# A hybrid decoder layer: another form for VectorE's two-tile operations, other durations for the planner's clocks

## The chip, the cores and the metric

The kernel runs on one core of a Trainium2 chip. A core has five engines that run side by side, each through its own queue in order: TensorE (PE, with its weight loads PEld), VectorE (DVE), ScalarE (ACT), GpSimd (POOL) and SyncE (SP, which here only issues transfers). They wait for each other through semaphores. The metric is the time of one execution on the device in microseconds (us), lower is better.

## The reference, cut to what matters

One layer for 256 tokens of width 2048, in float32. `rms_norm(x)` goes through one wide projection, whose columns feed two mixers; their outputs are merged by sigmoid gates, projected, and followed by a dense FFN of width 5632.

```
xn = rms_norm(h, ln_mix);  proj = xn @ w_in
q, k, v, z, b, a, sc_b, sc_c, sc_h, gate_a, gate_b = split(proj)
o_a = rms_norm(gated_delta(l2(silu(conv4(q,k))), silu(conv4(v)), decay(a), sigmoid(b))) * silu(z)
o_b = sc_b * conv3(sc_c * sc_h)
h = h + (sigmoid(gate_a) * (o_a @ w_proj_a) + sigmoid(gate_b) * (o_b @ w_proj_b)) @ w_out
h = h + (silu(rms_norm(h) @ w_gate) * (rms_norm(h) @ w_up)) @ w_down
return rms_norm(h, ln_final)
```

The gated delta rule (16 heads of 128) needs, in each head, the inverse of a unit-triangular matrix over the tokens.

## The kernel before, in words

**Products.** Every weight matrix is read once, in groups of 128 x 1024 numbers (two k-tiles of 512 columns). A group `raw` is loaded by SyncE; ScalarE makes its high part `wh` (a cast to float32r), VectorE the low part `wl = raw - wh`; a product is then three matmuls (hi x wh, lo x wh, hi x wl) for each k-tile and each of two token halves. So a group of weights feeds 12 matmuls of 512 columns, here called products; `wh63` is group 63 and feeds products 756 to 767, counted from the start. A projection of 512 columns is 96 products (`mm_k`, `mm_q`, ...), a result in two banks of PSUM. `ensure` makes the groups three ahead of their use.

**Order.** TensorE first makes k, q, v for head group 0, then for each further group k, the z of the group before, q, v; then the short convolution's scc, sch, scb (with z3 behind scc0), the gates and projections, out, and the FFN. What has to happen to a result (`post_qk`, `post_v`, `core`, ...) is written as generators that stop at every dependent step. `step` (line 329), called twice in each group of weights, runs those steps whose due time has come by the planner's own clocks. These are in `Pace` (line 52): one clock for each engine, advanced by an assumed duration for each instruction recorded through `Lane` (line 141) and by what its operands wait for. So the assumed durations decide behind how many products a step stands in each queue. They decide nothing on the chip: there an instruction waits in its queue until its semaphores allow it. When two results are still pending at the start of a product, `product` (line 372) forces steps ahead of their due time, whatever the clocks say, until one is evacuated.

**The DeltaNet steps of a head group** (four heads; the names carry the group's number). k and q are evacuated as rows, flipped to channels by 16 transposes on VectorE (fc), convolved (cv, 12 operations of VectorE), split into kh and kl, squared and split again (scv by ScalarE, sfc by VectorE), and summed by eight matmuls (ssb). Then, in `core` (line 809): the gram matmuls `gr0`, `gr1`, masked by VectorE into `ua`; the blocks of the diagonal are copied by ScalarE (c32), written to DRAM and read back in another layout by GpSimd's transfers (d0, ub); GpSimd inverts 32 x 32 blocks by forward substitution in 62 small operations (tb, rb); the result goes out and back (d1, rc); ScalarE copies rc into R, VectorE transposes parts of it (mt), and two levels of matmuls z and y complete the inverse. Then come u, uc, o, and oc, whose output `oa` is one mixer's result. Line 538, `hop`, issues the transfers, on GpSimd's queue.

**The end of the stage.** The evacuation of scb1 (`post_b`, line 1079) waits for the last oc, since its tiles take over memory of the DeltaNet stage.

Of the kernel before, what the change touches and what calls it, by code (L numbers as in the profile page):

```python
# [13 lines left out]
ALU = mybir.AluOpType  # L14
# [3 lines left out]
D = 2048  # L18
# [19 lines left out]
HOPE = 1  # L38
HOP = 2500.0
NOW = -2  # L40
# [11 lines left out]
class Pace:  # L52
    """Estimated engine clocks (ns), from each instruction's cost and the data it waits for."""

    RATE = {"act": (95.0, 0.84), "dve": (62.0, 1.045), "pool": (100.0, 2.25)}
    TABLE = {AF.Exp: 1, AF.Ln: 2, AF.Sigmoid: 3, AF.Silu: 4}
# [71 lines left out]
class Slots:  # L128
    """A tile pool that tells the clocks which tile takes over which slot."""

# [10 lines left out]
class Lane:  # L141
# [3 lines left out]
    def __getattr__(self, name):  # L145
        f = getattr(self.eng, name)
        pace, key = self.pace, self.key

        def call(*a, **k):
            aps = [v for v in (*a, *k.values()) if hasattr(v, "tensor")]  # L150
            out = k["out"] if "out" in k else a[0]
            outs = [out] + ([k["accum_out"]] if "accum_out" in k else [])
            ins = [v for v in aps if not any(v is o for o in outs)]
            n = math.prod(out.shape[1:])
            if name == "dma_start":
                pace.issue(key, 60.0, outs[:1], aps[1:], lag=HOP)
                return f(*a, **k)
            if key == "pe":
                rows = ins[0].shape[-1]
                if name == "transpose":  # L160
                    cyc = 2 * n
                elif ins[0].dtype == F32R:
                    cyc = max(n, 2 * rows)
                else:
                    cyc = 4 * max(n, rows, 32)
                pace.issue(key, cyc / 2.4 + 3.0, outs, ins)
                return f(*a, **k)  # L167
            if name == "tensor_reduce":
                n = math.prod(ins[0].shape[1:])
            cost, rate = Pace.RATE[key]  # L170
            if key == "pool" and name == "scalar_tensor_tensor":
                rate = 1.4
            cost += rate * n
            if key == "dve" and any(v.space == bass.MemoryType.PSUM for v in aps):
                cost += Pace.PSUM_COST
            if any(hasattr(k.get(nm), "tensor") for nm in ("scale", "scalar", "scalar1")):
                cost += Pace.SCALAR_COST
            func = a[2] if name == "activation" and len(a) > 2 else None
            table = Pace.TABLE.get(func, pace.table)
            if table != pace.table:  # L180
                pace.table = table
                cost += 1300.0
            pace.issue(key, cost, outs, ins)
            return f(*a, **k)  # L184

        return call
# [3 lines left out]
def tile_gdn_shortconv_layer(  # L190
# [23 lines left out]
    pace = Pace()  # L214
# [32 lines left out]
    def fetch(dst, src, free=0.0):  # L247
        """Load on the weights' queue."""
        nc.sync.dma_start(dst, src)
        start = max(pace.t["dma"], free)  # L250
        pace.t["dma"] = start + 4.0 * math.prod(dst.shape) / 360.0
        pace.note(dst, "dma", True, pace.t["dma"] + Pace.DMA_LAG)

    def pair(pool, tag, nm):
        t = pool.tile([P, 2, HG, T], F32R, tag=tag, name=nm)
        return t[:, 0], t[:, 1]

# [1 line left out]
    order = []  # L259
# [22 lines left out]
    def ensure(i, part=KGRP):  # L282
        while nxt[0] <= min(i, len(groups) - 1):
            n = nxt[0]
# [8 lines left out]
            for js in cuts:  # L293
                act.copy(wh[:, js, :], raw[:, js, :])
                if n < EARLY:
                    dve.tensor_tensor(wl[:, js, :], raw[:, js, :], wh[:, js, :], op=ALU.subtract)
                    continue
                lows.append((wl, raw, wh))
                if len(lows) > LOWLAG:
                    wl_, raw_, wh_ = lows.pop(0)  # L300
                    dve.tensor_tensor(wl_, raw_, wh_, op=ALU.subtract)
            ready[n] = (wh, wl)
            nxt[0] += 1
            if nxt[0] == len(groups):
                for wl_, raw_, wh_ in lows:
                    dve.tensor_tensor(wl_, raw_, wh_, op=ALU.subtract)

# [103 lines left out]

# [1 line left out]
    g_mix = const.tile([P, KD], F32, name="g_mix")  # L413
# [36 lines left out]
    def split(hi, lo, src, scale=None):  # L450
        if scale is None:
            act.copy(hi, src)
            dve.tensor_tensor(lo, src, hi, op=ALU.subtract)
        else:
            act.activation(hi, src, AF.Copy, scale=scale)
            dve.scalar_tensor_tensor(
                out=lo, in0=src, scalar=scale, in1=hi, op0=ALU.mult, op1=ALU.subtract
            )
# [65 lines left out]

# [1 line left out]

# [122 lines left out]
    def post_qk(g, qk, pt, me):  # L649
# [27 lines left out]
        yield  # L677
        dve.tensor_tensor(kq[1][:, :, qk, :], y, kq[0][:, :, qk, :], op=ALU.subtract)
        yield
# [6 lines left out]
        yield  # L686
        dve.tensor_tensor(sq[1], y, sq[0], op=ALU.subtract)
        yield 1
# [81 lines left out]
    def decay(g):  # L770
# [3 lines left out]

        # decay between token pairs, keys on partitions
        up_b = upper.unsqueeze(1).broadcast_to([P, HG, P])
# [32 lines left out]
    def core(g):  # L809
# [7 lines left out]

        # [keys, head, (kk, qk), block, queries]
        ua = gp.tile([P, HG, 2, 3, P], F32, tag="ua", name=f"ua_{g}")
# [33 lines left out]
        mark(("gram", g))  # L853
        # inverses of the unit-triangular 32-blocks: one block's every fourth row to a partition
        NM = 2 * HG
# [195 lines left out]

# [1 line left out]
    ob = [None] * NS  # L1053
# [25 lines left out]
    def post_b(n, pt, me):  # L1079
# [12 lines left out]
        yield from flip(rows, ch)  # L1092
        dve.tensor_tensor(y, y, ch, op=ALU.mult)
        yield SOON
# [23 lines left out]

# [1 line left out]
    while not late:  # L1120
# [8 lines left out]
    def post_m(n, br, pt, sg):  # L1129
        for m in range(2):  # L1130
            if br == 0:
                dve.tensor_tensor(mg[n][:, m, :], pt[m], sg[:, m, :], op=ALU.mult)
            else:
                dve.tensor_tensor(sg[:, m, :], pt[m], sg[:, m, :], op=ALU.mult)
                dve.tensor_tensor(mg[n][:, m, :], mg[n][:, m, :], sg[:, m, :], op=ALU.add)
        close(pt)
# [21 lines left out]

# [1 line left out]
    hg = [pair(apool, f"a{n}", f"hg{n}") for n in range(NS)]  # L1160
# [30 lines left out]

# [1 line left out]
    ff = []  # L1193
# [37 lines left out]
    def rsqrt_last(s0, s1, part, m):  # L1231
        """1 / sqrt(part + (s0 + s1) / D), one number to a partition."""
        t, h, y, u = (small.tile([P, 1], F32, tag=f"ry{i}", name=f"ry{i}{m}") for i in range(4))
# [17 lines left out]
    def post_y(n, m, pt):  # L1251
# [11 lines left out]
        if n < NS - 1:  # L1263
            dve.tensor_tensor(xh[:, m, cs], xh[:, m, cs], fin, op=ALU.mult)
            if n == NS - 2:
# [96 lines left out]
```

## Time and profile before

| | us |
|---|---|
| three runs | 1926.2, 1926.51, 1927.36 (median 1926.51) |
| span of the profiled execution | 1926.3 |
| TensorE busy | 1875.3 (97%) |
| VectorE busy | 1322.0 (69%) |
| ScalarE busy | 951.6 (49%) |
| GpSimd busy | 197.3 (10%) |

The profile tells of the profiled execution no time but its span, 0.2 us below the median of the runs. Busy TensorE is counted by the union of its matmuls, which overlap: one product is shown as 0.39 us long, while the next starts 0.23 us later. Idle time in front of an instruction is shown in brackets behind a row of a timeline, with what ended it; "L184" is the line of the helper that records every operation, so rows are told apart by their tiles, `out<-in`. In a timeline, neighbouring instructions of one kind are merged into one row (x2, x16).

### The profile page before, as it was taken

Reading aid. Unit: us, or ns where it says so; the run is one execution under the profiler, and the core shown is the slowest. Engines: PE = TensorE matmul, PEld = TensorE weight load, DVE = VectorE, ACT = ScalarE, POOL = GpSimd, SP = SyncE. Lnnn points to the kernel's source line nnn. Section 1 sums busy time; section 2 is a strip of 40 time slices with the busy share of each in tenths; the row PEclk is TensorE's granted clock in tenths of the full one; section 3 lists DMA queues with packets and bytes.
Section 4 is the critical chain, followed back from the end, with each engine's and each line's share of the span. In section 5 each row is a group of like instructions: output and inputs, shape, how many; then the busy total and the mean of one; then the engine's idle time right before and its main releaser. Section 6 shows DMA issues by size and latency. Waiting matters only on the chain.

```text
span 1926.3 us, 23591 instructions
## 1 busy us (share of the span) xinstructions
PE 1875.3 (97%) x8590; PEld 1543.4 (80%) x8590; DVE 1322.0 (69%) x1923; ACT 951.6 (49%) x1264; POOL 197.3 (10%) x352
## 2 busy tenths in 40 slices
PE   9999899997979999999999999999999999999998
PEld 7887687886867888888888888888888888888886
DVE  6899687896856778544466688766666666644454
ACT  6756766766544444444444444544444444444433
POOL 0007145172450000000000000000000000000000
PEclk9999999998989999999999999999999999999999
DMA  8556354363444655666655555566655555565553
GB/s 305 175 164 192 134 161 154 121 199 107 153 159 131 205 192 188 221 200 205 189 196 194 191 193 179 184 199 205 195 191 194 195 195 189 186 223 192 192 190 132
DMA packets 100357, 354.87 MB, mean 184 GB/s; under 512 B 12177, under 2 KB 12433, under 8 KB 99985
## 3 DMA queue, kind: packets, MB, share of 16 engines
q1 hardware_dynamic: 98432, 349.69, 55.1%
q0 software_dynamic: 1664, 3.67, 0.7%
q8 instruction: 67, 1.10, 0.2%
q14 instruction: 50, 0.40, 0.1%
q10 hardware_dynamic: 144, 0.01, 0.0%
HBM read 350.18 MB, written 3.15 MB: 183 GB/s over the span
## 4 chain that ended last, share of the span: by engine, by line
PE 80%; POOL 6%; issue 4%; DVE 4%; DMA 3%; ACT 2%; SPq 0%; POOLq 0%; DVEq 0%; ACTq 0%
PE mm_dn L167 13%; PE mm_fg L167 12%; PE mm_fu L167 12%; PE mm_proj L167 9%; PE mm_gate L167 9%; PE mm_out L167 5%; PE mm_scb L167 3%; PE mm_sch L167 3%; POOL tb L184 3%; PE mm_z L167 3%; POOL rb L184 2%; PE mm_q L167 2%; PE mm_scc L167 2%; PE mm_k L167 2%; PE mm_v L167 2%
## 5 line engine op out<-in xcount | busy, mean ns | idle before, releaser
L184 DVE TENSOR_TENSOR wl<-raw,wh 128x1024 fp32r<-128x1024 f32 (+1 forms) x652 | 793.1, 1229 | 503.7 <-ACT wh L184 498.8
L184 ACT CAST wh<-raw 128x1024 fp32r<-128x1024 f32 (+1 forms) x652 | 680.7, 1047 | 806.4 <-PE mm_fu L167 132.3
L167 PE MATMUL mm_dn<-wh,ff 128*128 128x512 f32 x704 | 219.0, 392 | 0.0
L167 PE MATMUL mm_fg<-wh,hg 128*128 128x512 f32 x704 | 216.7, 389 | 0.0
L167 PE MATMUL mm_fu<-wh,hg 128*128 128x512 f32 x704 | 216.7, 389 | 0.0
L167 PE MATMUL mm_gate<-wh,xg 128*128 128x512 f32 x512 | 157.6, 389 | 0.0
L167 PEld LDWEIGHTS mm_dn<-wh,ff 128*128 128x128 f32 x704 | 132.4, 188 | 29.5
L167 PEld LDWEIGHTS mm_fg<-wh,hg 128*128 128x128 f32 x704 | 132.2, 188 | 27.4
L167 PEld LDWEIGHTS mm_fu<-wh,hg 128*128 128x128 f32 x704 | 132.2, 188 | 27.3
L167 PE MATMUL mm_dn<-wl,ff 128*128 128x512 f32 x352 | 138.0, 392 | 0.0
L167 PE MATMUL mm_fg<-wl,hg 128*128 128x512 f32 x352 | 136.9, 389 | 0.0
L167 PE MATMUL mm_fu<-wl,hg 128*128 128x512 f32 x352 | 136.9, 389 | 0.0
L167 PEld LDWEIGHTS mm_gate<-wh,xg 128*128 128x128 f32 x512 | 96.1, 188 | 20.1
L167 PE MATMUL mm_gate<-wl,xg 128*128 128x512 f32 x256 | 99.7, 389 | 0.0
L167 PE MATMUL mm_z<-wh,xg 128*128 128x512 f32 x256 | 83.8, 409 | 0.0
L167 PE MATMUL mm_sch<-wh,xg 128*128 128x512 f32 x256 | 81.4, 399 | 0.0
L167 PE MATMUL mm_k<-wh,xg 128*128 128x512 f32 x256 | 79.4, 391 | 0.9 <-ACT wh L184 0.8
L167 PE MATMUL mm_out<-wh,m 128*128 128x512 f32 x256 | 80.1, 394 | 0.0
L167 PE MATMUL mm_proj<-wh,ob 128*128 128x512 f32 x256 | 79.9, 393 | 0.0
L167 PE MATMUL mm_q<-wh,xg 128*128 128x512 f32 x256 | 79.9, 393 | 0.0
L167 PE MATMUL mm_scc<-wh,xg 128*128 128x512 f32 x256 | 79.8, 393 | 0.0
L167 PE MATMUL mm_v<-wh,xg 128*128 128x512 f32 x256 | 79.2, 390 | 0.0
(247 smaller groups left out, 2879.6 us busy)
## 6 DMA issues: line engine op xcount, KB each, us to landing
raw<-in_w_in_dram SPq DMA_DIRECT2D x284, 512.0 KB, 4.2
raw<-in_w_gate_dram SPq DMA_DIRECT2D x88, 512.0 KB, 4.2
raw<-in_w_up_dram SPq DMA_DIRECT2D x88, 512.0 KB, 4.1
raw<-in_w_down_dram SPq DMA_DIRECT2D x88, 512.0 KB, 4.3
raw<-in_w_pb_dram SPq DMA_DIRECT2D x32, 512.0 KB, 4.3
raw<-in_w_pa_dram SPq DMA_DIRECT2D x32, 512.0 KB, 4.2
raw<-in_w_out_dram SPq DMA_DIRECT2D x32, 512.0 KB, 3.6
raw<-in_w_in_dram SPq DMA_DIRECT2D x8, 256.0 KB, 6.4
```

The source lines that it names most:

```text
L167: return f(*a, **k)
L184: return f(*a, **k)
```

## The change

There are two parts. First, where VectorE combined two tiles by a TENSOR_TENSOR operation in SBUF at the named places (wl above all, kl, sfc, the low parts of `split`, and three others), it now gets SCALAR_TENSOR_TENSOR with the constant 1.0 as its scalar: out = (a * 1.0) op b. Second, the planner's clocks get other durations: a transfer issued on GpSimd's queue occupies it for 650 ns instead of 60 and takes 3200 instead of 2500 ns more to land; GpSimd's operations 268 + 2.6 n ns instead of 100 + 2.25 n; VectorE's transposes 187 + 1.02 n instead of 62 + 1.045 n; memsets a rate of their own; a product 226.5 instead of 216.3 ns. What is computed stays the same.

```diff
-HOP = 2500.0
+HOP = 3200.0
+HOP_ISSUE = 650.0
-    RATE = {"act": (95.0, 0.84), "dve": (62.0, 1.045), "pool": (100.0, 2.25)}
+    RATE = {"act": (95.0, 0.84), "dve": (62.0, 1.045), "pool": (268.0, 2.6)}
+    TRANSPOSE = (187.0, 1.02)
+    MEMSET = (100.0, 0.86)
...
-                pace.issue(key, 60.0, outs[:1], aps[1:], lag=HOP)
+                pace.issue(key, HOP_ISSUE, outs[:1], aps[1:], lag=HOP)
...
-                pace.issue(key, cyc / 2.4 + 3.0, outs, ins)
+                pace.issue(key, cyc / 2.26, outs, ins)
...
-            if key == "pool" and name == "scalar_tensor_tensor":
-                rate = 1.4
+            if key == "dve" and name == "transpose":
+                cost, rate = Pace.TRANSPOSE
+            if name == "memset":
+                cost, rate = Pace.MEMSET
...
+    def both(out, a, b, op):
+        dve.scalar_tensor_tensor(out=out, in0=a, scalar=1.0, in1=b, op0=ALU.mult, op1=op)
+    def rest(lo, src, hi):
+        both(lo, src, hi, ALU.subtract)
...
-                    dve.tensor_tensor(wl_, raw_, wh_, op=ALU.subtract)
+                    rest(wl_, raw_, wh_)
...
-        dve.tensor_tensor(kq[1][:, :, qk, :], y, kq[0][:, :, qk, :], op=ALU.subtract)
+        rest(kq[1][:, :, qk, :], y, kq[0][:, :, qk, :])
...
-        dve.tensor_tensor(sq[1], y, sq[0], op=ALU.subtract)
+        rest(sq[1], y, sq[0])
...
-        dve.tensor_tensor(y, y, ch, op=ALU.mult)
+        both(y, y, ch, ALU.mult)
```

The second part moves instructions. The first z of head group 0 on TensorE stood before between weight groups 63 and 64; the last gr of that group stands in front of product 528 (group 44).

```order
L167 MATMUL mm0_k2_1766<-wl63_1871,xg3_135 128x512
L167 MATMUL mm1_k2_1767<-wh63_1870,xg3_135 128x512 x2
L167 MATMUL mm1_k2_1767<-wl63_1871,xg3_135 128x512
L167 MATMUL z_0_0_1995<-mt_141,ua_0_1279 32x32 x8
L167 MATMUL z_0_1_2006<-mt_141,ua_0_1279 32x32 x8
L167 MATMUL mm0_z1_2017<-wh64_1893,xg0_132 128x512 x2
L167 MATMUL mm0_z1_2017<-wl64_1894,xg0_132 128x512
```

The same place on TensorE in the changed program, where the last gr of the group stands in front of product 540 (group 45):

```order
L170 MATMUL mm0_q2_2204<-wl73_2083,xg0_132 128x512
L170 MATMUL mm1_q2_2205<-wh73_2082,xg0_132 128x512 x2
L170 MATMUL mm1_q2_2205<-wl73_2083,xg0_132 128x512
L170 MATMUL z_0_0_2230<-mt_141,ua_0_1297 32x32 x8
L170 MATMUL z_0_1_2241<-mt_141,ua_0_1297 32x32 x8
L170 MATMUL mm0_q2_2204<-wh73_2082,xg0_132 128x512 x2
L170 MATMUL mm0_q2_2204<-wl73_2083,xg0_132 128x512
```

So z moved from product 768 to product 882, the middle of group 73. Counted in the same way, the products between the last gr of a head group and its first z go from 240, 240, 246 and 234 to 342, 324, 294 and 312.

The sums of k3's squares, ssb_k3, on TensorE: before they stood inside scc0, in front of product 1452, with gr of head group 2 ending in front of product 1314.

```order
L167 MATMUL mm1_scc0_4009<-wl120_3943,xg0_132 128x512
L167 MATMUL ssb_k3_4029<-scv_k3_3987,sel_121 32x256 x4
L167 MATMUL ssb_k3_4029<-sfc_k3_3988,sel_121 32x256 x4
L167 MATMUL mm0_scc0_4008<-wh121_3962,xg0_132 128x512 x2
L167 MATMUL mm0_scc0_4008<-wl121_3963,xg0_132 128x512
```

In the changed program they stand between two results, with gr of head group 2 ending in front of product 1434:

```order
L170 MATMUL mm1_scc0_3893<-wl127_3989,xg3_135 128x512
L170 MATMUL ssb_k3_4155<-scv_k3_4151,sel_121 32x256 x4
L170 MATMUL ssb_k3_4155<-sfc_k3_4152,sel_121 32x256 x4
L170 MATMUL mm0_z3_4176<-wh128_4075,xg0_132 128x512 x2
L170 MATMUL mm0_z3_4176<-wl128_4076,xg0_132 128x512
```

They are now at product 1536, the last product of scc0 ahead of them and the first of z3 behind.

What feeds ssb_k3, on VectorE before, from the end of k3's convolution:

```order
L184 SCALAR_TENSOR_TENSOR cv_k3_3881<-fc_k3_3701,wc_123,cv_k3_3881 128x253 x2
L184 TENSOR_TENSOR wl119_3918<-raw119_3916,wh119_3917 128x1024
L184 TENSOR_TENSOR wl120_3943<-raw120_3941,wh120_3942 128x1024
L184 TENSOR_TENSOR kl_3_3699<-cv_k3_3881,kh_3_3698 128x4x256
L184 TENSOR_TENSOR wl121_3963<-raw121_3961,wh121_3962 128x1024
L184 TENSOR_TENSOR wl122_3982<-raw122_3980,wh122_3981 128x1024
L184 TENSOR_TENSOR sfc_k3_3988<-cv_k3_3881,scv_k3_3987 128x1024
```

And the same steps on VectorE in the changed program:

```order
L189 SCALAR_TENSOR_TENSOR cv_k3_3993<-fc_k3_3887,wc_123,cv_k3_3993 128x253 x2
L189 SCALAR_TENSOR_TENSOR wl129_4100<-raw129_4098,wh129_4099 128x1024
L189 SCALAR_TENSOR_TENSOR wl130_4125<-raw130_4123,wh130_4124 128x1024
L189 SCALAR_TENSOR_TENSOR kl_3_3885<-cv_k3_3993,kh_3_3884 128x4x256
L189 SCALAR_TENSOR_TENSOR sfc_k3_4152<-cv_k3_3993,scv_k3_4151 128x1024
```

The two wl between kl and sfc are gone from there. ScalarE's square of cv_k3 and its copy scv_k3 lie between kl and sfc in both programs.

Three other places: in GpSimd's queue the two multiplications of zs_2 now stand between the transfers d1_1 and rc_1 (before behind rc_1), and those of zs_3 between d1_2 and rc_2; the start of sch2 follows o1_3 on TensorE directly, with the evacuation of scc2 behind ScalarE's squares of o1_3; and the last oc, oc_3_1, moves from product 2010 to product 2250. Behind that TensorE's order is as before.

## Rows read from the trace of the kernel before

**Rows 1.** The page's first line.
```profile
span 1926.3 us, 23591 instructions
```
**Rows 2.** Busy time by stretch: stretch, length, engines' busy us, TensorE's clock, DMA.
```profile
0.00:604.40 604.40, 562.51 (x2831) 461.59 (x2832) 473.29 (x862) 379.14 (x654) 197.34 (x352) 0.97 0.50 166
604.40:1917.00 1312.60, 1312.60 (x5760) 1081.85 (x5759) 844.60 (x1046) 570.88 (x606) 0.00 (x0) 1.00 0.59 193
...
150.00:200.00 50.00, 46.43 (x209) 37.17 (x207) 47.96 (x79) 28.00 (x42) 36.52 (x75) 1.00 0.61 194
```
**Rows 3.** Chain that ended last: start us, us, what.
```profile
604.37 21.76 PE mm_scb L167 x96
```
**Rows 4.** Timeline of TensorE: start us, us, what [idle before, what ended it].
```profile
139.00 0.28 PE L167 MATMUL gr<-kl,kh 128*128 128x256 f32 x1
...
203.33 0.32 PE L167 MATMUL z<-mt,ua 128*32 128x32 f32 x2 [5.48 <-DVE mt L184]
...
206.15 1.22 PE L167 MATMUL mm_z<-wh,xg 128*128 128x512 f32 x2
...
208.88 0.76 PE L167 MATMUL dec<-gd,lower_r 128*128 128x512 f32 x2
...
261.49 0.28 PE L167 MATMUL gr<-kl,kh 128*128 128x256 f32 x1
...
322.29 0.28 PE L167 MATMUL z<-mt,ua 128*32 128x32 f32 x2 [2.95 <-DVE mt L184]
...
379.86 0.28 PE L167 MATMUL gr<-kl,kh 128*128 128x256 f32 x1
...
447.66 0.28 PE L167 MATMUL z<-mt,ua 128*32 128x32 f32 x2 [9.85 <-DVE mt L184]
...
500.13 0.28 PE L167 MATMUL gr<-kl,kh 128*128 128x256 f32 x1
...
562.69 0.28 PE L167 MATMUL z<-mt,ua 128*32 128x32 f32 x2 [9.21 <-DVE mt L184]
...
597.66 0.55 PE L167 MATMUL oc<-ident,zs 128*128 128x128 f32 x3 [1.65 <-POOL zs L184]
```
**Rows 5.** Timeline of VectorE, around cv_k1 and around k3's steps.
```profile
166.34 2.80 DVE L184 SCALAR_TENSOR_TENSOR cv_k<-fc_k,wc,cv_k 128x255 f32<-128x255 f32 x6
169.07 1.33 DVE L184 TENSOR_TENSOR wl<-raw,wh 128x1024 fp32r<-128x1024 f32 x1
...
382.98 0.86 DVE L184 SCALAR_TENSOR_TENSOR ua<-gr,s,em 128x256 f32<-128x256 f32 x2
...
409.98 1.32 DVE L184 TENSOR_TENSOR sfc_k<-cv_k,scv_k 128x1024 fp32r<-128x1024 f32 x1
```
**Rows 6.** Timeline of ScalarE: k3's square, copy and v3's evacuation; group 3.
```profile
407.68 1.05 ACT L184 ACTIVATE cv_k<-cv_k 128x1024 f32<-128x1024 f32 x1
408.76 1.05 ACT L184 CAST scv_k<-cv_k 128x1024 fp32r<-128x1024 f32 x1
...
413.11 1.26 ACT L184 ACTIVATE rows_v<-mm_v,rx 128x512 f32<-128x512 f32 x2
...
561.92 2.52 ACT L184 COPY R<-rc 32x128 f32<-32x128 f32 x8 [11.61 <-DMA rc<-d]
...
588.36 0.37 ACT L184 ACTIVATE jk<-o,rq 128x128 f32<-128x128 f32 x1 [0.31 <-PE o L167]
```
**Rows 7.** VectorE's groups by shape: count | busy us, mean ns | idle before.
```profile
L184 DVE TENSOR_TENSOR wl<-raw,wh 128x1024 fp32r<-128x1024 f32 x644 | 788.0, 1235 | 503.0 <-ACT wh L184 498.3
...
L184 DVE TENSOR_TENSOR mg<-mg,sg 128x512 f32<-128x512 f32 x8 | 5.5, 692 | 0.3
...
L184 DVE SCALAR_TENSOR_TENSOR xh<-xh,ry,lnf 128x512 f32<-128x512 f32 x2 | 1.5, 744 | 0.0
```
**Rows 8.** Timeline of GpSimd at 168 to 170 us.
```profile
168.51 0.35 POOL L184 TENSOR_TENSOR tb<-rb,ub 128x60 f32<-128x60 f32 x1
...
169.40 1.18 POOL L184 TENSOR_TENSOR tb<-rb,ub 128x76 f32<-128x76 f32 x1
```

More of the change, by code (lines that the diff above doesn't have):

```diff
@@ L295, in ensure @@
                 if n < EARLY:
-                    dve.tensor_tensor(wl[:, js, :], raw[:, js, :], wh[:, js, :], op=ALU.subtract)
+                    rest(wl[:, js, :], raw[:, js, :], wh[:, js, :])
                     continue
@@ L305, in ensure @@
                 for wl_, raw_, wh_ in lows:
-                    dve.tensor_tensor(wl_, raw_, wh_, op=ALU.subtract)
+                    rest(wl_, raw_, wh_)
     tasks = []
@@ L452, in split @@
             act.copy(hi, src)
-            dve.tensor_tensor(lo, src, hi, op=ALU.subtract)
+            rest(lo, src, hi)
         else:
@@ L1134, in post_m @@
                 dve.tensor_tensor(sg[:, m, :], pt[m], sg[:, m, :], op=ALU.mult)
-                dve.tensor_tensor(mg[n][:, m, :], mg[n][:, m, :], sg[:, m, :], op=ALU.add)
+                both(mg[n][:, m, :], mg[n][:, m, :], sg[:, m, :], ALU.add)
         close(pt)
@@ L1263, in post_y @@
         if n < NS - 1:
-            dve.tensor_tensor(xh[:, m, cs], xh[:, m, cs], fin, op=ALU.mult)
+            both(xh[:, m, cs], xh[:, m, cs], fin, ALU.mult)
             if n == NS - 2:
```

## The prediction

> **What bounds the kernel now.** I read the windows by stage first. From 604 to 1917 us TensorE is busy in every microsecond, at full clock [rows 2]; the chain of waits shows there nothing but products, 96 in 21.76 us, 0.2267 us each [rows 3]. Nothing that this change does can shorten that stretch, and it does not reorder TensorE there. Up to 604.4 us TensorE is busy for 562.5: 41.9 us stand idle, at a mean clock of 0.97 [rows 2]. That is all there is to win, plus what the lower clock costs.
>
> TensorE's own timeline says where the idle time is. Each of the four head groups has one large stop, always in front of the first z matmul: 5.48, 2.95, 9.85 and 9.21 us, together 27.5 [rows 4]. The row names VectorE's mt as what ended the wait, but mt only transposes R, and R is copied by ScalarE from rc, the last transfer of the round trip over GpSimd: ScalarE had stood 11.61 us for it in the last group [rows 6]. So the late one is the whole chain from the last gr matmul: mask and copy, d0 out, ub back, 62 small GpSimd operations, d1 out, rc back. From the end of the last gr to the first z it takes 203.33 - 139.28 = 64.1 us, then 60.5, 67.5 and 62.3 [rows 4]. Between the two the planner had put only 240, 240, 246 and 234 products, 53 to 56 us. After a stop TensorE is also slow: the six products from 206.15 to 208.88 take 2.73 us instead of 1.36 [rows 4].
>
> **The steps that are moved.** The order of the changed program gives, from last gr to first z, 342, 324, 294 and 312 products: 77.5, 73.4, 66.6 and 70.7 us. Against 64.1, 60.5, 67.5 and 62.3 us of chain, groups 0, 1 and 3 are covered with 8 to 13 us to spare. Group 2 is covered only because the ssb matmuls and a new stop (below) lie in the same stretch. Does the chain itself stay as long? Its largest part is the 62 GpSimd operations. A GpSimd operation takes about 0.35 us beside short VectorE operations, and 1.18 us when it meets a wl [rows 8, 5], but there is one wl for 12 products, and the changed program keeps that; so the count of long operations is bound to the time itself, and I take the chain as traced. In group 1 rc_1 now stands behind the two zs_2 multiplications in GpSimd's queue, and those wait for z2, whose products end 252 products (57.1 us) after the last gr; 16 us are then left for two multiplications, the transfer, the copies and mt. I price that at nothing; if it is late it costs TensorE one for one.
>
> So the four stops go: -27.5. The slow products behind them go too: 4 x 1.37 = -5.5. Of the remaining idle time before 604 us, 41.9 - 27.5 = 14.4, I take a little over a quarter as going with it, since part of it lies inside the z steps, where mt and zt run on a cold start: -4. Sum of the gains: -37.
>
> What is late next:
>
> The ssb matmuls of k3. In the new order they stand at the very end of scc0, in front of the first product of z3, 102 products (23.1 us) after the last gr of group 2; before there were 138. It is the place where `product` finds two results pending and forces the steps. What they need is VectorE's sfc_k3. Before, from the end of the last ua (383.84) to the end of sfc_k3 (411.30) VectorE worked 27.5 us without a pause [rows 5]. The new list has two wl fewer (-2.4), but they are those between kl and sfc, which hid ScalarE's square and copy of 1.05 us each [rows 6]: with nothing between, +2.1. That leaves 27.2. The last ua ended 3.7 us after gr; with less in front of it now, 1 to 3.7. TensorE has its 23.1 us: it waits 5.1 to 7.8 us; I take 6, by the lower end, since little stands in front of the last ua, and 1.4 for the slow products behind the wait: +7.4.
>
> The start of sch2. There, too, two results are pending, and scc2 is evacuated only after the four squares of o1_3 on ScalarE. Four squares at 0.37 us or somewhat more and half of an evacuation of 1.26 [rows 6]: 2.6 us in which TensorE waits. But this lies between o1_3 and oc_3, where TensorE waits already, 1.65 us for GpSimd's zs [rows 4], and that wait is covered by the new one: +1.
>
> Spacing within the groups. Where 12 to 30 products stood between two dependent steps of the chain from z to o, there are now mostly 6 (1.36 us). The last group ran with 6 before, and no gap beyond 0.3 us shows in it ahead of its oc. One wl in front of v on VectorE (1.24 us [rows 7]) is nearly all that 1.36 us holds. Between nothing and 1 us per group; I take 2 in all.
>
> **The two-tile operations.** 644 wl, and some dozens of others, change form. No row has the new form at 128x1024. From one side: SCALAR_TENSOR_TENSOR with a pointer for its scalar takes 744 ns at 128x512, TENSOR_TENSOR 692 [rows 7]: 52 ns more. With the constant 1.0 no pointer is read, so this is the upper end: 644 x 52 = 33 us of VectorE, of which only what falls in its full stretches (48.0 of 50 us from 150 to 200 [rows 2]) can reach TensorE, some 80 operations, 4 us. From the other side: if the new form does not hold up GpSimd, each wl that met a GpSimd operation, 1.33 us against 1.235 on the mean [rows 5, 7], gets 0.1 us shorter, 80 x 0.1 = 8 us of VectorE and 18 us of each GpSimd chain, of which TensorE sees the ssb_k3 wait shortened by 2 or 3. I take nothing, since the pointer is the nearest reason for the 52.
>
> The rows speak against that second end: beside cv_k in the SCALAR_TENSOR_TENSOR form a GpSimd operation of 60 elements takes 0.35 us, and the six VectorE operations 2.80 us [rows 8, 5]; the two alternate. The Trainium skill, "SBUF — State Buffer", section "Who interferes with whom", says that a VectorE instruction with two inputs in SBUF contends with a GpSimd instruction that reads SBUF, and makes no difference between the two forms. By that rule the GpSimd chain stays and the sum is 1899; by a form that leaves GpSimd alone it is some 3 us lower. No row here shows the rule for the new form at 1024 elements.
>
> **The sum.** -37 + 7.4 + 1 + 2 = -26.6, say -27. The profiled execution has a span of 1926.3 us [rows 1], 0.2 below the median of the three runs, so the same difference serves for both: 1926.5 - 27 = 1899 us.
>
> **Rivals.**
> A, the forecast: the four stops go, one new one comes; 1890 to 1906 us.
>
> B, VectorE takes over as the bound. For it: it is busy 48.0 of 50 us around the flips and convolutions [rows 2], and in all four groups ssb_q now follows ssb_k by 132 products, 29.9 us, into which flips, convolution, kl, sfc and eleven wl must go, about 29 us, more where GpSimd runs beside. Against it: before it kept up with 120 to 144 there. If seven such places (three ssb_k, four ssb_q) each wait 2 us, +14: 1913.
>
> C, the new form frees GpSimd: 1896, as above.
>
> D, slower. The last group's oc_3 moves back by 240 products, and scb1, which must wait for it, and with it scc2, scb2 and scc3 (flips, convolutions, splits) are pushed into the 438 products, 99 us, ahead of the first gate. VectorE owes there 36 wl of 1.235, 44 us, and some 45 us of these steps: 89 of 99. As long as that stays below 99 nothing happens; each us above is one us of TensorE, since ob is needed by the projections. To end slower than before it must eat the 27 us, that is run to 126 us, 1.4 times its rows. At 1.45 times: 1931.
>
> E, the change does not do what it says: the planner's clocks move the steps, but the chain moves along (rc behind zs, the GpSimd operations longer), the stops stay, and the time is 1926.
>
> **Chances.** A 0.60, B 0.22, C 0.08, D 0.05, E 0.05. About 0.2% (3.9 us) is what a measurement of this kernel can tell from no change. Faster by more: A, B, C, 0.89 with a little of B's far end gone to no change; no change 0.06, slower 0.05. The likeliest has 1890 to 1906. The range has to take in B above; below, no wait at ssb_k3 and 10 of the 14.4 us of small idle time gone (-33 - 10 + 3 = -40): 1886 to 1914.
>
> **What would show it.** Right: no gap above 1 us in front of any first z; ScalarE no longer idle for rc; one gap of 5 to 7 us in front of ssb_k3 at the end of scc0, and one of 2 to 3 us at the first product of sch2; TensorE's end of the DeltaNet stage some 27 us earlier, and the stretch after it as long as before. wl at 1.22 to 1.26 us. Wrong: gaps of 2 us or more before many ssb (B); GpSimd operations of 0.3 us beside a wl (C); a stop at the projections of the first branch (D); z still waiting for mt (E).

## The result, and the profile after

| | before | after |
|---|---|---|
| median of the runs, us | 1926.93 (4 runs) | 1896.05 (4 runs, 1895.1 to 1897.37) |
| ratio after / before | | 0.9841, 95% interval 0.9829 to 0.9853 |
| span of the profiled execution, us | 1926.3 | 1893.7 |
| TensorE busy / idle in the span, us | 1875.3 / 51.0 | 1868.0 / 25.7 |

The changed kernel is 31 us faster; 1899 was forecast. The span is 32.6 us shorter: TensorE idles 25.3 us less, and its matmuls take 7.3 us less, since fewer of them run at the low clock. In every run on record the span is 1.7 to 2.2 us below the time of the same execution. So the profiled execution before was one of about 1928 us, longer than the median and not 0.2 us below it, and that is what lies between 32.6 and 31. In the table of the experiments hop6000 stands with two of its four runs (1906.75 and 1908.86 us), since the other two took over 3,100 at a granted clock of 0.66 and 0.56.

The first lines of the page of the changed kernel, against [rows 1]:

```profile
span 1893.7 us, 23598 instructions
...
PE 1868.0 (99%) x8590; PEld 1538.5 (81%) x8590; DVE 1322.7 (70%) x1923; ACT 954.0 (50%) x1264; POOL 196.3 (10%) x352
```

The windows, against [rows 2] (columns as there):

```profile
0.00:604.40 604.40, 590.48 (x2979) 486.05 (x2980) 497.69 (x885) 392.75 (x654) 193.39 (x350) 0.99 0.54 179
612.60:1885.00 1272.40, 1271.98 (x5576) 1047.60 (x5576) 818.79 (x1022) 553.73 (x586) 2.95 (x2) 1.00 0.59 192
150.00:200.00 50.00, 50.00 (x230) 41.48 (x229) 48.83 (x79) 31.87 (x46) 36.41 (x76) 1.00 0.61 198
```

Up to 604 us TensorE is busy 28 us longer than before; after the DeltaNet stage it is full, as before: from product 2256 to the end of the last one it takes 1258.6 us in both kernels. VectorE is still nearly full from 150 to 200 us (48.83 of 50), and there TensorE no longer waits for anything.

TensorE's timeline at the first z of the four groups, against [rows 4], with the first products behind it in group 0:

```profile
224.15 1.20 PE L170 MATMUL z<-mt,ua 128*32 128x32 f32 x32
225.28 0.73 PE L170 MATMUL mm_q<-wh,xg 128*128 128x512 f32 x2
...
346.58 0.69 PE L170 MATMUL z<-mt,ua 128*32 128x32 f32 x16
...
469.34 0.69 PE L170 MATMUL z<-mt,ua 128*32 128x32 f32 x16
...
586.83 1.20 PE L170 MATMUL z<-mt,ua 128*32 128x32 f32 x32
```

No row has an idle time behind it: the four stops, 27.5 us, are gone. The 32 z themselves are shorter too: in group 0 from 224.15 to 225.28, 1.13 us, where before they took 2.82 (203.33 to 206.15). Those three microseconds by windows, before and after, show TensorE's clock (third figure from the end) at its lower level, 1.2 GHz, behind the stop, and at 2.4 GHz without one:

```profile
203.30:206.30 3.00, 2.41 (x33) 2.08 (x33) 2.57 (x8) 2.87 (x8) 0.00 (x0) 0.50 0.00 0
```
```profile
224.10:227.10 3.00, 3.00 (x41) 2.61 (x41) 2.79 (x7) 2.95 (x6) 2.29 (x3) 1.00 0.17 70
```

ScalarE's copy of rc into R in the last group, against the 11.61 us of waiting in [rows 6]: the data are there when ScalarE comes to them.

```profile
583.58 2.52 ACT L189 COPY R<-rc 32x128 f32<-32x128 f32 x8
```

TensorE's remaining stops of more than 0.6 us in its timeline, in order of time (one of 1.44 us at the kernel's very start is left out; it is there before too):

```profile
329.06 0.73 PE L170 MATMUL mm_q<-wh,xg 128*128 128x512 f32 x2 [1.77 <-ACT zs L189]
...
419.31 1.06 PE L170 MATMUL ssb_k<-scv_k,sel 128*32 128x256 f32 x4 [4.28 <-ACT scv_k L189]
420.72 1.06 PE L170 MATMUL ssb_k<-sfc_k,sel 128*32 128x256 f32 x4 [0.35 <-DVE sfc_k L189]
...
446.39 0.72 PE L170 MATMUL mm_sch<-wh,xg 128*128 128x512 f32 x2 [1.50 <-ACT zs L189]
...
508.42 0.66 PE L170 MATMUL vt<-ident,cv_v 128*128 128x128 f32 x4 [1.43 <-DVE ua L189]
...
612.52 1.22 PE L170 MATMUL mm_sch<-wh,xg 128*128 128x512 f32 x2 [2.66 <-ACT scc L189]
```

With one more vt, 1.09 us in group 1, these are 13.1 of the 25.7 us; 9.1 more lie behind the last product, as before. The second and third rows and the last are the two stops that were foreseen, ssb_k3 and the start of sch2. The two in front of mm_q (329.06) and mm_sch (446.39) were not foreseen: the result of z2 (z3) has just ended, its place in PSUM is wanted at once, and its evacuation zs stands on ScalarE behind steps of cv_q (square, kh, scv) and casts.

What leads to ssb_k3 on VectorE and ScalarE, against [rows 5, 6]:

```profile
391.94 0.88 DVE L189 SCALAR_TENSOR_TENSOR ua<-gr,s,em 128x256 f32<-128x256 f32 x2 [0.40 <-PE gr L170]
...
415.74 1.35 DVE L189 SCALAR_TENSOR_TENSOR kl<-cv_k,kh 128x1024 fp32r<-128x1024 f32 x1
419.29 1.37 DVE L189 SCALAR_TENSOR_TENSOR sfc_k<-cv_k,scv_k 128x1024 fp32r<-128x1024 f32 x1 [2.20 <-ACT scv_k L189]
```
```profile
417.13 1.06 ACT L189 ACTIVATE cv_k<-cv_k 128x1024 f32<-128x1024 f32 x1 [1.03 <-DVE kl L189]
418.21 1.04 ACT L189 CAST scv_k<-cv_k 128x1024 fp32r<-128x1024 f32 x1
```

From the end of the last ua, 392.82, to that of sfc_k3, 420.66, lie 27.8 us (forecast 27.2). With no wl left between kl and sfc, VectorE stands 2.20 us for ScalarE's square and copy (forecast 2.1).

The new form, against [rows 7, 8]: VectorE's group by shape, and a GpSimd operation beside a wl.

```profile
L189 DVE SCALAR_TENSOR_TENSOR wl<-raw,wh 128x1024 fp32r<-128x1024 f32 x644 | 787.9, 1233 | 473.3 <-ACT wh L189 467.8
```
```profile
166.76 1.19 POOL L189 TENSOR_TENSOR rb<-rb,tb 128x66 f32<-128x66 f32 x1
```

A wl takes 1233 ns instead of 1235, and a GpSimd operation that meets one takes 1.19 us (the next one, beside the next wl, 1.16), as before.

### The profile page after: what moved, and what is told of

The parts are those of the page before. It is cut to its first block, busy times and chain, and to the rows that moved or that the text cites. A ratio compares the mean times of both kernels' runs of the same rounds, so it can differ in the third digit from the quotient of the medians.

```text
span 1893.7 us, 23598 instructions
## 1 busy us (share of the span) xinstructions
PE 1868.0 (99%) x8590; PEld 1538.5 (81%) x8590; DVE 1322.7 (70%) x1923; ACT 954.0 (50%) x1264; POOL 196.3 (10%) x352
## 4 chain that ended last, share of the span: by engine, by line
PE 94%; DVE 3%; ACT 2%; issue 1%; DMA 0%; SPq 0%; DVEq 0%; ACTq 0%
PE mm_dn L170 13%; PE mm_fg L170 13%; PE mm_fu L170 13%; PE mm_proj L170 9%; PE mm_gate L170 9%; PE mm_out L170 5%; PE mm_v L170 4%; PE mm_k L170 4%; PE mm_scb L170 4%; PE mm_z L170 4%; PE mm_scc L170 4%; PE mm_sch L170 4%; PE mm_q L170 4%; DVE wl L189 1%; PE gr L170 1%
## 5 line engine op out<-in xcount | busy, mean ns | idle before, releaser
L189 DVE SCALAR_TENSOR_TENSOR wl<-raw,wh 128x1024 fp32r<-128x1024 f32 (+1 forms) x652 | 793.1, 1226 | 473.6 <-ACT wh L189 468.0
L170 PE MATMUL mm_scb<-wh,xg 128*128 128x512 f32 x256 | 80.1, 394 | 0.0
L170 PE MATMUL mm_z<-wh,xg 128*128 128x512 f32 x256 | 79.9, 394 | 0.0
```

## The experiments

The products between the last gr of a head group and its first z are called cover here. They are counted in TensorE's order; a product lasts 0.2267 us [rows 3]. A "first z" is the first one of its head group, and HOP is the planner's constant for how long a transfer takes to land. The reference time of the kernel before lay between 1924.8 and 1926.9 in all comparisons.

| kernel | cover of the four groups | us | ratio to before, 95% |
|---|---|---|---|
| stt_only | 240, 240, 246, 234 | 1925.95 | 1.0000 (0.9992 to 1.0009) |
| clocks_only | 342, 324, 294, 312 | 1894.08 | 0.9840 (0.9826 to 0.9853) |
| pool_clocks | 342, 336, 324, 330 | 1909.74 | 0.9921 (0.9907 to 0.9934) |
| pe_clocks | 234, 234, 228, 228 | 1952.57 | 1.0140 (1.0125 to 1.0156) |
| hop3200 | 258, 270, 264, 258 | 1924.03 | 0.9994 (0.9985 to 1.0003) |
| hop4500 | 306, 300, 300, 294 | 1886.91 | 0.9800 (0.9787 to 0.9813) |
| hop5000 | 324, 312, 306, 318 | 1895.95 | 0.9847 (0.9832 to 0.9861) |
| hop6000 | 342, 342, 330, 342 | 1906.75, 1908.86 | 0.9908 (0.9888 to 0.9928) |
| z3_first | 342, 324, 330, 312 | 1892.24 | 0.9825 (0.9812 to 0.9838) |
| after_again | 342, 324, 294, 312 | 1896.61 | 0.9850 (0.9836 to 0.9863) |
| after_hop2500 | 300, 300, 306, 306 | 1887.06 | 0.9803 (0.9790 to 0.9817) |
| wl_halves | 240, 240, 246, 234 | 1912.83 | 0.9935 (0.9918 to 0.9952) |

### The two parts apart

**stt_only**: the new form with the old durations.
```diff
-dve.tensor_tensor(wl_, raw_, wh_, op=ALU.subtract)
+dve.scalar_tensor_tensor(out=wl_, in0=raw_, scalar=1.0, in1=wh_, op0=ALU.mult, op1=ALU.subtract)
```


> The two-tile operations in the new form, in the order of the kernel before on every engine. Theory (the form is worth nothing): 1926.5 us, within 2; the four z stops stay at 5.5, 3.0, 9.9 and 9.2 us, wl at 1.23 us. Rival C (the new form frees GpSimd): the 62 small operations take some 18 us less in each group, the z stops go, 1900 to 1905. Rival (the form costs 52 ns in each of 644 wl where VectorE is full): 1929 to 1931, wl at 1.28 us.

1925.95 us, the theory; the z stops are 6.57, 1.08, 9.51 and 8.98 us, wl takes 1236 ns. GpSimd's 248 substitution operations, by line (count | busy us, mean ns | idle before):

```profile
L189 POOL TENSOR_TENSOR tb<-rb,ub 128x60 f32<-128x60 f32 (+24 forms) x124 | 64.7, 522 | 26.6 <-DMA ub<-d 17.2
L189 POOL TENSOR_TENSOR rb<-rb,tb 128x60 f32<-128x60 f32 (+24 forms) x124 | 62.9, 507 | 9.7
```

Together 127.6 us. The same two rows of the kernel before:

```profile
L184 POOL TENSOR_TENSOR tb<-rb,ub 128x60 f32<-128x60 f32 (+24 forms) x124 | 67.0, 540 | 28.3 <-DMA ub<-d 18.9
L184 POOL TENSOR_TENSOR rb<-rb,tb 128x60 f32<-128x60 f32 (+24 forms) x124 | 61.0, 492 | 9.7
```

Together 128.0 us. The form neither costs VectorE anything nor frees GpSimd. Rival C is out.

**clocks_only**: the new durations, with `both` written as `dve.tensor_tensor(out, a, b, op=op)`.

> The durations of the changed program, so its order on every engine, with TENSOR_TENSOR as before. Theory (the order is everything): 1896 us, within 2. Rival C: the GpSimd operations beside a wl get longer again, the wait for ssb_k3 with it, 1899 to 1903. Rival (the new form costs VectorE something): 1892 to 1894, shorter than the changed kernel.

1894.08 us, and the ratio of the changed kernel; its ssb_k3 stop is 4.29 + 0.59 us. In the traces the operations of each engine follow each other as in the changed kernel (and in stt_only as in the kernel before). The whole gain is the order's.

### Which durations

**pool_clocks**: the new durations of transfers, GpSimd and memsets alone. It is the changed kernel with the old durations of products and transposes:
```diff
-    TRANSPOSE = (187.0, 1.02)
+    TRANSPOSE = (62.0, 1.045)
...
-                pace.issue(key, cyc / 2.26, outs, ins)
+                pace.issue(key, cyc / 2.4 + 3.0, outs, ins)
```
**pe_clocks**: the new durations of products and transposes alone. It is the changed kernel with the old durations of the rest:
```diff
-HOP = 3200.0
-HOP_ISSUE = 650.0
+HOP = 2500.0
+HOP_ISSUE = 60.0
...
-    RATE = {"act": (95.0, 0.84), "dve": (62.0, 1.045), "pool": (268.0, 2.6)}
+    RATE = {"act": (95.0, 0.84), "dve": (62.0, 1.045), "pool": (100.0, 2.25)}
...
-    MEMSET = (100.0, 0.86)
+    MEMSET = (100.0, 2.25)
```


> New form; of the durations only those for transfers, GpSimd's operations and memsets are the new ones, products and transposes keep the old ones. From last gr to first z stand 342, 336, 324 and 330 products. Theory (what is counted for the round trip over GpSimd decides how far z is put off): no stop in front of any z, 1893 to 1899; ssb_k3 still at product 1536, 102 products behind gr, with its stop of 4 to 5 us. Rival (product and transpose durations are needed as well): z stops of 2 us or more stay, 1905 or more.

> New form; of the durations only those for products and transposes are the new ones, GpSimd's stay. From last gr to first z stand 234, 234, 228 and 228 products, 6 to 18 fewer than before; 180 from gr to ssb_k, and no step is forced. Theory: the z stops stay and grow by the missing products, 5.5+1.4, 3.0+1.4, 9.9+4.1, 9.2+1.4 = 35.8 us, no stop for ssb_k3; 1930 to 1936. Rival (the gain comes from steps that are better spaced, not from the z stops): 1900 to 1915.

pool_clocks: 1909.74 us, the rival's time, but not for the rival's reason. The z stops go but for 1.06 us in group 1, as the theory has it; but ssb_k3 stands only 78 products behind gr in this order (the 102 of the expectation were a mistake), and other places stop:

```profile
422.83 1.06 PE L170 MATMUL ssb_k<-scv_k,sel 128*32 128x256 f32 x4 [7.81 <-ACT scv_k L189]
...
451.45 1.22 PE L170 MATMUL mm_sch<-wh,xg 128*128 128x512 f32 x2 [3.53 <-ACT zs L189]
```

So cover was bought, and half of the changed kernel's gain is missing (16 of 32 us). GpSimd's queue shows one thing more: d1_2 (`d<-rb`) stands behind zs_2, which waits for ScalarE.

```profile
451.48 2.97 POOL L189 TENSOR_TENSOR zs<-zs,ng 128x512 f32<-128x512 f32 x2 [7.62 <-ACT zs L189]
454.40 2.35 POOL L160 DMA_DIRECT2D d<-rb  x4
```

The last rb of that group had ended at 443.86, so its round trip is over 10 us longer for a place in a queue; only the large cover hid it.

pe_clocks: 1952.57 us, worse than the theory's 1930 to 1936. The stops between gr and z are there, 10.21, 10.66, 7.94 and 9.82 us, together 38.6 (forecast 35.8), but in two groups in front of dec (matmuls on the decay gd, which stand near z). Further stops of 1.65 to 3.4 us came elsewhere (for zs, and at oc and ssb_q): in all TensorE idles 18.6 us more than before and is busy 7.6 longer. Why dec stops, on TensorE and ScalarE:

```profile
207.78 0.80 PE L170 MATMUL dec<-gd,lower_r 128*128 128x512 f32 x1 [10.21 <-ACT gd L189]
```
```profile
202.96 2.52 ACT L189 COPY R<-rc 32x128 f32<-32x128 f32 x8 [11.33 <-DMA rc<-d]
...
206.45 2.44 ACT L189 ACTIVATE gd<-upper,gdec_rf 128x128 fp32r<-128x128 f32 x8
```

ScalarE waits at R for rc, and gd, which needs nothing of rc, stands behind R in ScalarE's queue. The row blames gd; what was late is rc.

### How much cover

The kernel before with one number changed:
```diff
-HOP = 2500.0
+HOP = 4500.0      # 3200, 5000, 6000
```


> The kernel before with a transfer taken to land after 3200 ns instead of 2500, as in the changed kernel, and nothing else. From last gr to first z stand 258, 270, 264 and 258 products: 18, 30, 18 and 24 more than before, worth 4.1, 6.8, 4.1 and 5.4 us. Theory: the stops shrink one for one, 5.5, 3.0, 9.9, 9.2 to 1.4, 0, 5.8, 3.8, together 11; 1926 - 16.5 - 1.4 for the slow products behind one stop = 1908. Rival (the chain is stretched as z is put off, since more VectorE work falls beside GpSimd): stops stay near 25 us, 1920 or more.

> The kernel before, TENSOR_TENSOR and all, with one number changed: a transfer is taken to land 4500 ns after its issue instead of 2500. From last gr to first z stand 306, 300, 300 and 294 products (before 240, 240, 246, 234), ssb_k3 stands 126 products behind gr of group 2 and inside scc0, no step is forced. Theory (the stops in front of z are the whole loss, and any duration that puts z off far enough takes them away): 69.4, 68.0, 68.0 and 66.6 us of products against chains of 64.1, 60.5, 67.5 and 62.3 us, so no stop of 1 us or more before a z, no stop of 4 us at ssb_k3 and none at sch2; 1926 - 33 = 1893, or 1889 with the small idle time that the changed kernel lost too. Rival (the gain needs the durations as traced, of transposes, products and GpSimd, and comes from the better spacing of all steps): z stops gone, but other stops in their place, 1900 to 1915.

> The kernel before with a transfer taken to land after 5000 ns, nothing else: from last gr to first z 324, 312, 306 and 318 products; ssb_k3 120 products behind gr, at product 1536 but not forced; scc's evacuation forced at the start of sch2. Theory: no stop before z, 0 to 1.5 us at ssb_k3, 1 to 2.7 at sch2, with the oc stop of 1.7 us gone: 1887 to 1890. Rival (any cover above the chain is as good): 1885 to 1887.

> The kernel before with a transfer taken to land after 6000 ns, nothing else: from last gr to first z 342, 342, 330 and 342 products, as far as in the changed kernel or farther; as there ssb_k3 is forced at product 1536 (108 products behind gr, 102 there), and steps of head group 3 and scc are forced at the start of sch2. Theory (cover beyond the chain is paid back where results pile up): no stop before z, a stop of 3 to 4.5 us at ssb_k3 and of 2 to 3 us at sch2, 1893 to 1897, the changed kernel's time and not that of 4500 ns. Rival (the changed kernel loses its 10 us to the other durations, not to the longer cover): 1886 to 1889.

hop3200: a miss, 1924.03 us. There are 18 to 30 products more of cover, and the stops are together as long as before: 5.37, 10.08, 6.42 and 7.13 us, 29.0 against 27.5. The one of group 1:

```profile
336.86 0.79 PE L167 MATMUL dec<-gd,lower_r 128*128 128x512 f32 x1 [10.08 <-ACT gd L184]
```
```profile
330.89 2.52 ACT L184 COPY R<-rc 32x128 f32<-32x128 f32 x8 [9.55 <-DMA rc<-d]
...
335.54 2.44 ACT L184 ACTIVATE gd<-upper,gdec_rf 128x128 fp32r<-128x128 f32 x8
```

Two things ate the cover in that group. The chain is longer: from the last gr to the copy of R 68.2 us instead of 59.8 (the 62 GpSimd operations take 39.9 us instead of 35.1). And dec now stands in front of z, with gd behind R on ScalarE: TensorE resumes 6.0 us after the start of the copy, where before z followed it after 0.8. In groups 0 and 2 it was dec alone: their chains to the copy did not grow (63.2 and 62.3 us, before 63.4 and 66.7), and TensorE resumes 4.8 and 6.0 us after the copy's start. In group 3 z still follows after 0.8, and the chain grew by 3.4 us, to 64.9. So the rival's time came, and half of its reason.

hop4500: 1886.91 us, faster than the theory said and 9.7 us faster than the changed kernel beside it (after_again), by one number, without the new form. No stop in front of a first z or its dec exceeds 0.7 us, and ssb_k3 does not stop:

```profile
215.01 1.20 PE L167 MATMUL z<-mt,ua 128*32 128x32 f32 x32
...
402.01 0.63 PE L167 MATMUL ssb_k<-scv_k,sel 128*32 128x256 f32 x4
...
443.98 1.20 PE L167 MATMUL z<-mt,ua 128*32 128x32 f32 x32
```

TensorE is busy 1864.3 and idle 19.9 us in a span of 1884.2: both below the changed kernel's 1868.0 and 25.7.

hop5000 (1895.95) and hop6000 (1907) are slower again. Both expectations named the direction and were too low. Both had also said that no z would stop, but in both z of group 1 does, 2.29 and 1.45 us in spite of 312 and 342 products. There the round trip is not what is late. In hop5000 rc had landed at 331.17, but ScalarE came to R at 335.56, and mt stood on VectorE behind wl and the eight transposes of v (fc_v):

```profile
335.56 2.53 ACT L184 COPY R<-rc 32x128 f32<-32x128 f32 x8
...
342.99 1.96 DVE L184 STREAM_TRANSPOSE mt<-R 32x128 f32<-32x128 f32 x6
```

In hop6000 rc had landed 13 us before ScalarE copied it (327.31 and 340.27). hop6000's longest stops are at the start of sch, of sch2 and of scb:

```profile
446.44 1.22 PE L167 MATMUL mm_sch<-wh,xg 128*128 128x512 f32 x2 [4.49 <-ACT zs L184]
...
605.65 0.72 PE L167 MATMUL mm_sch<-wh,xg 128*128 128x512 f32 x2 [4.03 <-ACT scc L184]
...
643.75 0.79 PE L167 MATMUL mm_scb<-wh,xg 128*128 128x512 f32 x2 [3.68 <-DVE scc L184]
```

These are places where a new result waits for the evacuation of an older one: cover beyond the chain comes back there. At ssb_k3, where 3 to 4.5 us were expected, it waits 1.5. Against hop4500, TensorE idles 14.8 us more in hop6000 and is busy 5.6 us more, 10.1 of its busy us at the lower clock, where hop4500 has none. For hop5000, which besides z stops at sch (2.08), sch2 (1.50) and oc (1.65, twice), it is 4.7 us of idle and 6.4 of busy time, with 10.2 at the lower clock.

### The changed kernel, with its forced stops taken away

**z3_first**: z3 ahead of scc0. **after_again**: the changed kernel once more. **after_hop2500**: the changed kernel with HOP put back.
```diff
+    product_z(NG - 1)                  # z3_first, ahead of the loop over scc
-        if n == 0:
-            product_z(NG - 1)
```
```diff
-HOP = 3200.0
+HOP = 2500.0                           # after_hop2500
```


> The changed kernel with the projection for z3 ahead of scc0 instead of behind it, in TensorE's order and in that of the loads. From last gr to first z stand 342, 324, 330 and 312 products; ssb_k3 stands 126 products behind gr of group 2, inside scc0, and is no longer forced; the start of sch2 still is. Theory (ssb_k3 stops TensorE because the forced place leaves it 23 us for some 28 us of VectorE and ScalarE work): that stop of 4.6 us with the slow products behind it goes, 1889 to 1891, 5 to 7 us below the changed kernel. Rival (VectorE is short of time there in any case, the stop moves to another ssb or to v): within 2 us of the changed kernel.

> The changed kernel once more, beside the others on the same chip: 1894 to 1897 us, stops as in its first profile within 0.5 us.

> The changed kernel with one number put back: a transfer lands 2500 ns after its issue as in the kernel before, not 3200. From last gr to first z stand 300, 300, 306 and 306 products (changed kernel 342, 324, 294, 312); ssb_k3 stands 126 products behind gr, inside scc0, and is not forced; the start of sch2 still is. Theory (the changed kernel loses its 10 us against the 4500 ns version to cover beyond the chain, which pushes ssb_k3 to a forced place): no stop of 1 us or more before z, none of 3 us or more at ssb_k3, sch2 2.7 us: 1888 to 1892. Rival (it loses them to the other durations, transposes and GpSimd's, whatever the cover): 1894 to 1897. Rival (300 products are too few for the chain of this order): z stops of 2 to 5 us, 1897 or more.

after_again came as expected (1896.61 us; its ssb_k3 stop is 4.14 us). z3_first: 1892.24 us against 1896.61 beside it, 4.4 us, short of the theory's 5 to 7 and more than the rival's 2. The stop at ssb_k3 is gone, but oc_3, whose wait sch2's had covered, stops again, and vt of the last group waits 2.35 us instead of 1.43:

```profile
417.09 0.73 PE L170 MATMUL mm_scc<-wh,xg 128*128 128x512 f32 x2 [1.71 <-ACT zs L189]
...
422.71 0.63 PE L170 MATMUL ssb_k<-scv_k,sel 128*32 128x256 f32 x4
...
600.19 0.72 PE L170 MATMUL mm_sch<-wh,xg 128*128 128x512 f32 x2 [1.21 <-ACT scc L189]
...
624.77 0.70 PE L170 MATMUL oc<-ident,zs 128*128 128x128 f32 x3 [1.65 <-POOL zs L189]
```

after_hop2500: 1887.06 us, a little below the theory's 1888 to 1892, and the other durations are those of the change. Its first z have no stop, ssb_k3 has none, and sch2 has one of 1.49 us:

```profile
212.89 1.20 PE L170 MATMUL z<-mt,ua 128*32 128x32 f32 x32
...
408.68 0.63 PE L170 MATMUL ssb_k<-scv_k,sel 128*32 128x256 f32 x4
...
608.68 0.73 PE L170 MATMUL mm_sch<-wh,xg 128*128 128x512 f32 x2 [1.49 <-ACT scc L189]
```

So the changed kernel loses its 9 to 10 us against the best versions to the order that the longer cover (342 and 324 products in its first two groups) brings, not to its other durations: two quite different sets of durations that give 294 to 306 products give 1887.

### The chain itself

**wl_halves**: the kernel before, in its order, with wl in two instructions (the planner is charged the same for the two as for the one).
```diff
-dve.tensor_tensor(wl_, raw_, wh_, op=ALU.subtract)
+for j in range(KGRP):
+    dve.tensor_tensor(wl_[:, j, :], raw_[:, j, :], wh_[:, j, :], op=ALU.subtract)
```


> The kernel before, in its order on every engine, with each two-tile wl of 128x1024 written as two operations of 128x512 (1235 ns against 2 x 688 by the rows of before). Theory (a small GpSimd operation that meets a wl is held to the end of that one instruction, and gets its turn between the two halves): beside a wl 0.65 to 0.75 us instead of 1.18; the 62 operations take 5 to 9 us less than 35.7, 35.1, 39.4 and 37.0; the z stops of 5.5, 3.0, 9.9 and 9.2 us shrink to about 0, 0, 3 and 2; 1900 to 1908. Rival (it is held by the bytes that VectorE moves, whatever the instruction): chains as before or some us longer, since VectorE works 0.1 us more for each wl; 1926 to 1932.

1912.83 us: the mechanism is the theory's, the gain smaller (13 instead of 18 to 26). The timeline of GpSimd beside four halves in a row (two of its four operations there), and its two rows by line:

```profile
164.57 0.63 POOL L187 TENSOR_TENSOR tb<-rb,ub 128x66 f32<-128x66 f32 x1
165.27 0.66 POOL L187 TENSOR_TENSOR rb<-rb,tb 128x66 f32<-128x66 f32 x1
```
```profile
L187 POOL TENSOR_TENSOR rb<-rb,tb 128x60 f32<-128x60 f32 (+24 forms) x124 | 56.5, 456 | 9.7
L187 POOL TENSOR_TENSOR tb<-rb,ub 128x60 f32<-128x60 f32 (+24 forms) x124 | 53.0, 427 | 26.6 <-DMA ub<-d 17.2
```

Together 109.5 us instead of 128.0, so 4.6 us less in each chain, just under the expected 5 to 9. VectorE pays 46 us more over the kernel (1368.3 instead of 1322.0), and ssb_k, which waits for it, stops up to 1.7 us in three groups; the z stops are 1.54, 0.3, 4.10 and 6.85.

## Why the prediction was right, point by point

**The bound and the four z stops: right.** 27.5 us of stops were to go, and went. That they were the round trip's, and not mt's, is shown by ScalarE's waits at R (before, pe_clocks, hop3200) and by hop4500, which removes them with one number for the transfers.

**The chain as traced: right on the whole, not group by group.** The GpSimd operations take 127.9 us in the changed kernel against 128.0. From the end of the last gr to rc's landing it takes 61.6, 66.1, 60.4 and 64.7 us, before 63.3, 59.7, 66.7 and 61.4. In group 1 rc_1, behind the two zs_2, is issued 9.9 us after the last rb instead of 5.1; "I price that at nothing" held because the changed kernel had 9.3, 6.8, 12.4 and 2.7 us to spare, from rc's landing to ScalarE's copy. Where there is nothing to spare a longer chain costs TensorE, as "one for one" warned: hop3200's chain in group 1 is 8 us longer. pool_clocks's, 10 us longer for d1's place behind zs, was hidden.

**Cold products: right, too small.** -5.5 was put for the products behind the stops. The 32 z of each group run at the low clock too: 2.82, 2.73, 2.67 and 2.73 us before, 1.13 to 1.24 after (from first z to next product, less what stands between). By the stretches in which the granted clock is 0.50, TensorE is busy at that clock for 22.4 us before (19.0 of them behind the four z stops, 3.4 behind oc_3's) and for 8.0 after (4.9 around ssb_k3, 3.2 at sch2). A product takes twice its time there, so half of this is lost: 9.5 us behind the z stops, where the sum had 5.5, and 2.4 around ssb_k3, where it had 1.4. The difference, 11.2 - 4.0 = 7.2, is all but 0.1 us of the fall of busy time.

**Small idle: mis-sized.** -4 was taken, a little over a quarter of 14.4 us. Worked out: 51.0 - 27.5 = 23.5 us of other idle before, 25.7 - 13.1 = 12.6 after, so -10.9, with oc_3's stop in it (9.2 without). In both kernels 9.1 us of it lie behind the last product, so three quarters of the 14.4 went.

**ssb_k3: right in place and cause, shorter than the 5 to 7 us named as its sign.** 6 us were forecast at the end of scc0, and 4.63 (4.28 + 0.35) came. TensorE was there at 415.04, 23.1 us after gr as forecast, and VectorE's stretch was 27.8 instead of 27.2, but the last ua ended 0.9 us behind gr, not 1 to 3.7. sfc_k3 was ready 5.6 us after TensorE came, and 1.06 of these TensorE worked on the four ssb matmuls that need scv alone, which the sum had left out. z3_first shows that the forced place makes the stop.

**sch2 and oc_3: right.** 2.66 us against 2.6, and oc_3's wait is hidden behind it; z3_first shows both halves, since there the one shrinks to 1.21 and the other is back.

**Spacing and stops elsewhere: only in part.** +2 stood for spacing; vt waits 2.5 us in two groups (0.90 in one before). The two zs stops, 3.3 us, were not in the sum.

**The form: right.** 0 was taken, stt_only says 0 within 0.1%, and both ends (+4 us; 3 us less) fell. The Trainium skill, "SBUF — State Buffer", section "Who interferes with whom", says that a VectorE instruction with two inputs in SBUF contends with a GpSimd instruction that reads SBUF; for the new form at 1024 elements the trace now agrees, 1.16 to 1.19 us beside a wl.

**The sum.** Idle: forecast -27.5 - 4 + 6 + 1 + 2 = -22.5, measured -27.5 - 10.9 + 13.1 = -25.3. Busy: forecast -5.5 + 1.4 = -4.1, measured -7.3. Together -26.6 was forecast and -32.6 of span measured. With oc_3's 1.65 us booked at sch2, as the sum had it, small idle gave 5.2 us more than forecast and cold products 3.2, and the new stops cost 2.4 more (11.4 instead of 9). That these offset each other in part is luck. Of the rivals, B has no stops of its kind (one ssb stops, at the foreseen place), and D has no stop at the first branch's projections (its 1931 would be 1929 by its own numbers: 1.45 times 89 us is 129, 30 above 99).

What stays open: where between 270 and 294 products the stops vanish was not tried, and apart from HOP no duration was changed alone.

## What to carry to other kernels

Where a planner's clocks place dependent steps, what counts is not that the durations are true but how many products they put between two ends of a chain: too few show as a stop at the step, too many as stops where results pile up. Of the covers tried here the best, 294 to 306 products, lies just above the chain's length. Before such a number is trusted, sweep it: one constant was worth more (38 us) than the whole set as traced (31 us). And when a stop names an engine, look at what stands ahead in that engine's queue: gd, zs and d1 were each late only because of their neighbour.

## What the runs showed that was not expected

A GpSimd operation that meets a wl is held for the rest of that one VectorE instruction. All tb and rb that start while a wl is running end 0.08 to 0.22 us behind it: 48 in the kernel before, 51 in the changed one, 82 in wl_halves. Beside 128x1024 the middle one of them takes 1.17 us (before) and 1.16 (after), beside 128x512 0.63. Cutting the instruction in two gave GpSimd its turn in between, with VectorE paying 2 x 699 instead of 1235 ns.
